# Retention of a hybrid decoder step: own accumulator banks, a third projection bank, and transposes moved into the gate's projection

## The chip, the cores and the metric

One core of a Trainium2 chip. The metric is the device time of one execution in microseconds (us). Engines are called as the profile calls them: PE (matrix products and transposes), PEld (loading of PE's weights), DVE, ACT, POOL, and SP, which issues most DMAs.

## What is computed

One decoder layer on 1,024 prompt tokens and 8 x 4 sample tokens (1,056 token columns in all), float32, width 1,024. The normed input is projected to 6,468 columns; these feed a sparse attention, which picks 256 keys per query by an indexer's scores, and in parallel a retention with 8 heads of 64; both are gated, merged and projected out. The part at stake is retention, per head (lg is the head's log decay, chunks of 128 tokens):

```
scores = einsum('bihd,bjhd->bhij', q, k) * dmat
out = einsum('bhij,bjhe->bihe', scores, v)
out = out + einsum('bihd,bhde->bihe', q, state) * q_decay
new_state = exp(lg * C) * state + einsum('bjhd,bjhe->bhde', k * k_decay, v)
y_r = group_norm_heads(out) * g_ret * silu(zr)
```

## The kernel before, in words

The projection runs in blocks of 128 columns of w_in. `project` takes a block's weights, split by ACT (L195) and DVE or POOL (L196) into a high and a low part, and makes three chunks of 352 tokens; a chunk is 24 products (8 slices of the width x 3 terms, lines 209 to 211) into one PSUM bank, which a function `use` then empties on ACT or DVE. These chunks take two banks by turns (`pj`), so a chunk can start when the one before the last has been emptied.

`retention` goes through four pairs of heads. For each it projects keys, queries (both rotated), values and the gate z; then the attention queries (`split_rows`: ACT L446 and DVE L447 make a high and a low part of each chunk, and after the third chunk ACT L451 copies its last 32 columns to `qs`), then two blocks of merging gates (`gates`, ACT L643). PE has its instructions interleaved by a scheduler that works on the program's order, on data and on `issue_after`, which forbids an instruction to be placed ahead of another.

Inside `pair`: values and keys are turned to tokens (`to_tokens`: 9 transposes each into `pt`, emptied by ACT, L524 and L527). `kd` and `vtok` give the states (L545), a scan on DVE (`S`, L547), two copies on ACT into `SD` (L549). Query-key products go into `pl` (L556), and DVE multiplies them with the decay (`tmp`, L561, 1,024 columns). SD times queries (L568) and values times `tmp` (L571) add up in `po`, which ACT copies (L577), PE turns (L581), ACT copies (L582). The sample tokens do the same in small (L594 to L605, `ss` on DVE, L596). Group norm follows: mean on DVE (L614), a subtraction on POOL (L617), squares on ACT (L619), the rest on DVE and POOL, and three more blocks of transposes (L633).

`pl` is two tiles of two banks each, `pt` two banks, `pj` two: all eight of PSUM.

While PE goes through gates and retention, DVE and ACT search for the 256th largest score (`pick_all`): 31 rounds, one per bit of the threshold. In a round DVE counts five score tiles (L795), ACT counts two by signs (L802: 1,024 columns of 128 rows, then `scs`, the sample's 1,056), DVE makes the bit (L809, L811), the threshold (L871) and the next candidate (`cand`, L873), on which the next counts wait. Their work is in the same two queues as retention's.

```
def count_signs(thr):
    for j, (sc, bi, n, W) in enumerate(AB):
        ...
        nc.scalar.activation(junk[:n, :W], sc, AF.Sign, bias=thr[:n, NV + j:NV + j + 1], scale=-1.0,
```

Of the kernel before, what the change touches and what calls it, by code (L numbers as in the profile page):

```python
# [8 lines left out]
F32 = mybir.dt.float32  # L9
# [108 lines left out]
def _hybrid_step(ctx, tc, A, outs, dbg):  # L118
# [292 lines left out]
    def project(f0, use, chunks=chunks):  # L411

        if not split:
            prefetch()
        g0, w = split.pop(0)
        assert g0 == f0
        prefetch()
        for c, sl in enumerate(chunks):
            p = pj()[:, :sl.stop - sl.start]
            for k in range(KT):  # L420
                terms(p, w, k, sl)
            use(c, p)

    back = []

# [14 lines left out]
    def split_rows(pool, f0, p, dst, new, x=None):  # L440

        hl = [pool.tile([128, TT], F32R, name="raw", bufs=2) for _ in "hl"]

        def use(c, y):
            sl = slice(c * CH, c * CH + CH)
            nc.scalar.copy(hl[0][:, sl], y)  # L446
            nc.vector.tensor_sub(hl[1][:, sl], y, f32(hl[0][:, sl]))  # L447
            if x is not None:
                nc.scalar.copy(x[:, sl], y)
            if c == 2:  # L450
                nc.scalar.copy(new[:, p], y[:, CH - NS:])  # L451
        project(f0, use)
# [7 lines left out]
    def retention(gp):  # L460
        with ExitStack() as s3:
            rp = s3.enter_context(tc.tile_pool(name="rp", bufs=1, reuse_waits="tile"))
            RC = rp.tile([128, R_ALL], F32, name="rc")
            nc.sync.dma_start(RC, A["rcs"])
            O = rp.tile([128, 9, 2, 64], F32, name="O")
            nc.gpsimd.memset(O[:, 8], 0.0)
            SD = rp.tile([128, 8, 128], F32, name="SD")
            nc.gpsimd.memset(SD, 0.0)
            for p in range(4):
                pair(rp, RC, O, SD, p)  # L470
                split_rows(gp, O_QA + 128 * p, p, QD, qs)
                gates(gp, (4 + 2 * p, 5 + 2 * p))

    def big(rp, name):
# [1 line left out]

    def to_tokens(src, use):

        for g in range(3):
# [7 lines left out]
    def pair(rp, RC, O, SD, p):  # L487
# [64 lines left out]

        sT = []
        for g in (0, 1):
            px = pl()
            together([lambda c=c, i=i: nc.tensor.matmul(px[:, 512 * i + 128 * c:512 * i + 128 * c + 128],  # L556
                                                        kT[head[i], 512 * g + 128 * c:512 * g + 128 * c + 128],
                                                        qT[head[i], 512 * g + 128 * c:512 * g + 128 * c + 128], start=True, stop=True)
                      for c in range(4) for i in (0, 1)])
            t = flat(big(rp, "tmp"))[:, :1024].rearrange("p (i c x) -> p i c x", i=2, c=4)  # L560
            nc.vector.tensor_tensor(t, px.rearrange("p (i c x) -> p i c x", i=2, c=4),  # L561
                                    DM[:, M_D:M_D + 256].rearrange("p (i x) -> p i x", i=2).unsqueeze(2).to_broadcast([128, 2, 4, 128]),
                                    op=OP.mult)
            sT.append(t)


        po = pl()
        together([lambda c=c: nc.tensor.matmul(po[:, 128 * c:128 * c + 128], SD[:, c - 1], qT[:, 128 * c:128 * c + 128],  # L568
                                               start=(c % 4 == 3), stop=False) for c in range(7, 0, -1)])
        for g in (0, 1):  # L570
            together([lambda c=c, i=i: nc.tensor.matmul(po[head[i], 128 * c:128 * c + 128], vtok[:, c, head[i]], sT[g][:, i, c % 4],  # L571
                                                        start=False, stop=(c % 4 == 3))
                      for c in range(4 * g, 4 * g + 4) for i in (0, 1)])
        oT = flat(big(rp, "tmp"))[:, :1024]
        for g in (0, 1):
            half = slice(512 * g, 512 * g + 512)
            nc.scalar.copy(oT[:, half], po[:, half])  # L577
            x = pt()
            for j in range(4):
                c0 = 512 * g + 128 * j  # L580
# [11 lines left out]
        px = pl()  # L592
        for i in (0, 1):
            nc.tensor.matmul(px[:NS, 512 * i:512 * i + 32], kT[head[i], T:], qT[head[i], T:], start=True, stop=True)  # L594
        ss = rp.tile([NS, 64], F32, name="ss")
        nc.vector.tensor_tensor(ss.rearrange("p (i t) -> p i t", i=2), px[:NS].rearrange("p (i t) -> p i t", i=2)[:, :, :32],  # L596
                                DM[:NS, M_S:M_S + 64].rearrange("p (i t) -> p i t", i=2), op=OP.mult)
        pi = pl()
        together([lambda b=b, i=i: nc.tensor.matmul(pi[:NS, 512 * i:512 * i + 64], qm[head[i], b], ST0[head[i], b], start=(b == 0), stop=False)
                  for b in range(NB) for i in (0, 1)])  # L600
        for i in (0, 1):
            nc.tensor.matmul(pi[:NS, 512 * i:512 * i + 64], ss[:, 32 * i:32 * i + 32], vtok[:NS, 8, head[i]], start=False, stop=True)
        nc.scalar.copy(O[:NS, 8], pi[:NS].rearrange("p (h e) -> p h e", h=2)[:, :, :64])
# [45 lines left out]
    with ExitStack() as s1:  # L649
# [412 lines left out]
        past_scores(G)  # L1062
    for p in range(4):
        x = tl.tile([128, TT], F32, name="kx", bufs=1)
        split_rows(tl, O_KA + 128 * p, p, KD, ks, x)
# [323 lines left out]
```

## Time and profile before

| | us |
|---|---|
| median of 3 runs | 1141.44 (1141.26 to 1142.6) |
| the profiled execution | 1139.63 |
| its span, first to last instruction | 1137.8 |
| PE busy | 1089.7 (96%) |
| DVE busy | 679.5 (60%) |
| ACT busy | 471.1 (41%) |
| POOL busy | 226.2 (20%) |

Read it so: the four pairs of retention lie between about 165 and 555 us of the span; the head before them loads inputs and makes the scores, the attention follows. A busy share is a mean over these stages. PE's time counts a product until its modelled end, so two products that overlap in the pipe are not counted twice. A wait is the idle time ahead of an instruction, with the instruction that ended it.

### The profile page before, as it was taken

Reading aid. Unit: us, or ns where it says so; the run is one execution under the profiler, and the core shown is the slowest. Engines: PE = TensorE matmul, PEld = TensorE weight load, DVE = VectorE, ACT = ScalarE, POOL = GpSimd, SP = SyncE. Lnnn points to the kernel's source line nnn. Section 1 sums busy time; section 2 is a strip of 40 time slices with the busy share of each in tenths; the row PEclk is TensorE's granted clock in tenths of the full one; section 3 lists DMA queues with packets and bytes.
Section 4 is the critical chain, followed back from the end, with each engine's and each line's share of the span. In section 5 each row is a group of like instructions: output and inputs, shape, how many; then the busy total and the mean of one; then the engine's idle time right before and its main releaser. Section 6 shows DMA issues by size and latency. Waiting matters only on the chain.

```text
span 1137.8 us, 20198 instructions
## 1 busy us (share of the span) xinstructions
PE 1089.7 (96%) x7978; PEld 986.6 (87%) x7978; DVE 679.5 (60%) x1637; ACT 471.1 (41%) x910; POOL 226.2 (20%) x194
## 2 busy tenths in 40 slices
PE   6989999999989999999999999999989999999997
PEld 5779788899879999999989999777989888898886
DVE  6775369999999865943223122101357767588645
ACT  6574355654565332232233322211336666443111
POOL 0012015023310311012332212143013333100000
PEclk9999999999999999999999999999999999999999
DMA  9933334135233524422876676596899741483321
GB/s 311 229 89 94 101 113 133 41 108 153 80 91 108 151 77 131 130 61 78 275 253 211 218 222 175 187 312 225 278 267 256 197 111 31 156 269 118 116 93 56
DMA packets 157237, 179.32 MB, mean 158 GB/s; under 512 B 18821, under 2 KB 129101, under 8 KB 156054
## 3 DMA queue, kind: packets, MB, share of 16 engines
q1 hardware_dynamic: 147208, 142.31, 42.4%
q0 software_dynamic: 9856, 35.66, 9.7%
q8 instruction: 63, 1.03, 0.4%
q14 instruction: 32, 0.26, 0.1%
q10 hardware_dynamic: 78, 0.06, 0.0%
HBM read 137.23 MB, written 36.98 MB: 153 GB/s over the span
## 4 chain that ended last, share of the span: by engine, by line
PE 74%; DVE 12%; DMA 5%; ACT 4%; issue 3%; SPq 1%; DVEq 0%; ACTq 0%
PE pj L209 13%; PE pj L211 13%; PE pj L210 13%; DVE eq L795 4%; PE po L1173 3%; PE pj L1327 3%; PE pj L1326 3%; PE pj L1325 3%; PE str L1014 2%; PE tr L1156 2%; PE pj L949 2%; PE pj L950 2%; PE pj L951 2%; ACT ra L802 2%; PE sx L1042 1%
## 5 line engine op out<-in xcount | busy, mean ns | idle before, releaser
L209 PE MATMUL pj<-hh,wh 128*128 128x352 f32 (+1 forms) x1168 | 384.5, 329 | 10.8 <-ACT qs L451 4.4
L211 PE MATMUL pj<-hh,wl 128*128 128x352 f32 (+1 forms) x1168 | 378.8, 324 | 0.0
L210 PE MATMUL pj<-hl,wh 128*128 128x352 f32 (+1 forms) x1168 | 378.2, 324 | 0.0
L209 PEld LDWEIGHTS pj<-hh,wh 128*128 128x128 f32 x1168 | 220.1, 188 | 20.7 <-issue 8.1
L211 PEld LDWEIGHTS pj<-hh,wl 128*128 128x128 f32 x1168 | 219.9, 188 | 4.8 <-issue 4.1
L210 PEld LDWEIGHTS pj<-hl,wh 128*128 128x128 f32 x1168 | 220.8, 189 | 2.9 <-issue 2.5
L795 DVE TENSOR_SCALAR_CACHE_REDUCE eq<-sc,cand 128x896 bf16<-128x896 f32 (+4 forms) x155 | 135.6, 875 | 2.4
L195 ACT CAST wh<-ws 128x1024 fp32r<-128x1024 f32 (+1 forms) x65 | 61.1, 941 | 115.6 <-PE pj L210 67.7
L196 DVE TENSOR_TENSOR wl<-ws,wh 128x1024 fp32r<-128x1024 f32 (+1 forms) x48 | 51.8, 1082 | 59.3 <-ACT wh L195 59.2
L196 POOL TENSOR_TENSOR wl<-ws,wh 128x1024 fp32r<-128x1024 f32 x17 | 41.4, 2437 | 166.9 <-ACT wh L195 166.7
L1143 POOL TENSOR_SCALAR lg<-lg,st 128x1024 f32<-128x1024 f32 (+7 forms) x64 | 48.2, 759 | 121.6 <-DVE st L1142 73.2
L802 ACT ACTIVATE ra<-sc,cand 128x1024 bf16<-128x1024 f32 x31 | 35.7, 1151 | 59.7 <-DVE cand L873 58.7
L1141 ACT ACTIVATE lg<-lg,st 128x1024 f32<-128x1024 f32 (+7 forms) x64 | 49.5, 775 | 24.7 <-DVE st L1140 22.5
L1016 DVE COPY kt<-str 128x512 f32<-128x512 f32 x32 | 22.1, 690 | 61.2 <-PE str L1014 57.6
L643 ACT ACTIVATE raw<-pj 128x352 f32<-128x352 f32 x48 | 22.2, 462 | 77.7 <-PE pj L211 74.5
L1325 PE MATMUL pj<-woh,MH 128*128 128x512 f32 (+1 forms) x136 | 51.3, 377 | 0.0
L1326 PE MATMUL pj<-wol,MH 128*128 128x512 f32 (+1 forms) x136 | 51.2, 377 | 0.0
L1327 PE MATMUL pj<-woh,ML 128*128 128x512 f32 (+1 forms) x136 | 51.2, 377 | 0.0
L984 POOL DMA_INDIRECT kv<-in_cache_k,idx x32 | 31.0, 968 | 98.5 <-PE str L1014 79.8
L984 POOL DMA_INDIRECT kv<-in_cache_v,idx x32 | 31.1, 972 | 74.5 <-PE sx L1042 45.4
L1156 PE MATMUL tr<-C,lg 128*128 128x128 f32 x288 | 44.5, 276 | 1.2 <-DVE pT L1158 0.3
L1156 PEld LDWEIGHTS tr<-C,lg 128*128 128x128 f32 x288 | 33.7, 140 | 9.5 <-issue 2.4
(352 smaller groups left out, 1956.3 us busy)
## 6 DMA issues: line engine op xcount, KB each, us to landing
ws<-in_w_in SPq DMA_DIRECT2D x51, 512.0 KB
TG<-raw SPq DMA_DIRECT2D x16, 528.0 KB
rot<-in_rot SPq DMA_DIRECT2D x8, 1056.0 KB
x<-in_w_ada SPq DMA_DIRECT2D x16, 512.0 KB
u<-TG SPq DMA_DIRECT2D x8, 528.0 KB
t<-TG SPq DMA_DIRECT2D x8, 528.0 KB
x<-in_x_prompt SPq DMA_DIRECT2D x8, 512.0 KB
out<-tk SPq DMA_DIRECT2D x16, 256.0 KB
```

Source lines behind the costliest of these rows:

```text
L195: nc.scalar.copy(wh[:, :, :n], ws[:, :, :n])
L196: (nc.vector if k == 4 or len(order) % 3 else nc.gpsimd).tensor_sub(wl[:, :, :n], ws[:, :, :n], f32(wh[:, :, :n]))
L209: nc.tensor.matmul(p, wh[:, k], HH[k][:, sl], start=(k == 0), stop=False)
L210: nc.tensor.matmul(p, wh[:, k], HL[k][:, sl], start=False, stop=False)
L211: nc.tensor.matmul(p, wl[:, k], HH[k][:, sl], start=False, stop=(k == KT - 1))
L795: nc.vector.tensor_scalar(junk[:n, :W], sc, thr[:n, j:j + 1], 0.0, op0=op, op1=OP.add, accum_out=cnt[:n, j:j + 1])
L802: nc.scalar.activation(junk[:n, :W], sc, AF.Sign, bias=thr[:n, NV + j:NV + j + 1], scale=-1.0, accum_out=cnt[:n, NV + j:NV + j + 1])
L984: nc.gpsimd.indirect_dma_start(out=t.rearrange("p s c -> p (s c)"), out_offset=None, in_=cache.rearrange("g (r s) h d -> (g r) (s h d)", s ...
L1156: nc.tensor.transpose(x[:, 128 * (j - j0):128 * (j - j0) + 128], lg[:, j % 2, 128 * (j // 2):128 * (j // 2) + 128], ident)
L1325: nc.tensor.matmul(x, MH[:, k, tk], wh[:, k], start=(k == 0), stop=False)
L1326: nc.tensor.matmul(x, MH[:, k, tk], wl[:, k], start=False, stop=False)
L1327: nc.tensor.matmul(x, ML[:, k, tk], wh[:, k], start=False, stop=(k == KT - 1))
```

## The change

Before retention the pool with `pl` and `pt` is closed and one with two `pt`, three single accumulator banks `pb` and one bank `pj3` is opened. `two()` gives two of the `pb`. Every third chunk of a projection takes `pj3`. A double-width tile becomes two single ones, so that its reader on DVE or ACT becomes two instructions. Transposes of values and keys, a group of up to four at a time, stand behind the chunks of z's projection: both large groups of the values behind the first chunk, their small one and the first of the keys behind the second, the rest behind the third. The first chunk of the attention queries' projection now stands ahead of SD's products. Lines of the new file carry other numbers: L451 is L469, L446 L464, L549 L578, L547 L576, L561 L591, L596 L630, L568 L601, L577 L610, L619 L653, L643 L677, L802 L836, L811 L845, L809 L843, L871 L905, L873 L907, L795 L829, L196 L205, L195 L204, L538 L562, L527 L552.

```
+    third, turns = [None], [0]
     def pj():
+        turns[0] += 1
+        if third[0] and turns[0] % 3 == 0:
+            return third[0].tile([128, 512], F32, name="pj3", bufs=1)
         return psj.tile([128, 512], F32, name="pj", bufs=2)
+    def two():
+        return [ps.tile([128, 512], F32, name="pb", bufs=3) for _ in (0, 1)]
...
+    def project_parts(f0, use, chunks=chunks):
...
+            end = last_on(mybir.EngineType.PE)
             use(c, p)
+            yield end
...
             for p in range(4):
-                pair(rp, RC, O, SD, p)
-                split_rows(gp, O_QA + 128 * p, p, QD, qs)
+                rows = split_rows(gp, O_QA + 128 * p, p, QD, qs)
+                pair(rp, RC, O, SD, p, rows)
+                for _ in rows:
+                    pass
...
-        to_tokens(raw(O_VR + 128 * p, "tmp"), use_v)
-        to_tokens(kT, use_k)
+        vT = raw(O_VR + 128 * p, "tmp")
...
-        project(O_ZR + 128 * p, use_z)
+        blocks = [x for a in (turned(vT, use_v), turned(kT, use_k)) for x in (a, a, a)]
+        for c, end in enumerate(project_parts(O_ZR + 128 * p, use_z)):
+            with tc.issue_after(end):
+                for x in blocks[2 * c:2 * c + 2]:
+                    next(x)
...
-            px = pl()
+            px = two()
...
-            nc.vector.tensor_tensor(t, px.rearrange("p (i c x) -> p i c x", i=2, c=4),
...
+            for i in (0, 1):
+                nc.vector.tensor_tensor(t[:, i], px[i].rearrange("p (c x) -> p c x", c=4),
+                                        DM[:, M_D + 128 * i:M_D + 128 * i + 128].unsqueeze(1).to_broadcast([128, 4, 128]), op=OP.mult)
...
-        po = pl()
...
+        end = next(rows)
+
+        po = two()
+        by_bank = lambda c: slice(128 * (c % 4), 128 * (c % 4) + 128)
+        with tc.issue_after(end):
+            together([lambda c=c: nc.tensor.matmul(po[c // 4][:, by_bank(c)], SD[:, c - 1], qT[:, 128 * c:128 * c + 128],
+                                                   start=(c % 4 == 3), stop=False) for c in range(7, 0, -1)])
...
+            nc.scalar.copy(oT[:, half], po[g])
...
+        px = two()
...
+        for i in (0, 1):
+            nc.vector.tensor_tensor(ss[:, 32 * i:32 * i + 32], px[i][:NS, :32], DM[:NS, M_S + 32 * i:M_S + 32 * i + 32], op=OP.mult)
+        pi = two()
...
+        for i in (0, 1):
+            nc.scalar.copy(O[:NS, 8, i], pi[i][:NS, :64])
...
         gates(gp, range(4))
+        ps1.close()
+        ps1 = ExitStack()
+        ps = third[0] = ps1.enter_context(tc.tile_pool(name="psr", bufs=1, reuse_waits="tile", space=PSUM))
         retention(gp)
         drain()
...
+    third[0] = None
     ps1.close()
```

ACT's queue behind pair 1, in round 25 of the search, before (`raw` is the attention queries' high part, then the gates' rows; `sc` and `scs` are the two sign passes):

```order
L195 CAST wh<-ws 128x1024
L446 CAST raw<-pj 128x352
L802 ACTIVATE ra,cnt<-sc_787,cand 128x1024
L451 COPY qs<-pj 128x32
L619 ACTIVATE tmp<-O 128x1152
L802 ACTIVATE ra,cnt<-scs,cand 32x1056
L643 ACTIVATE raw<-pj 128x352 x2
```

and the same place in the change (`pj_3118` is the third bank):

```order
L204 CAST wh<-ws 128x1024
L464 CAST raw<-pj_3118 128x352
L836 ACTIVATE ra,cnt<-sc_787,cand 128x1024
L836 ACTIVATE ra,cnt<-scs,cand 32x1056
L653 ACTIVATE tmp<-O 128x1152
L469 COPY qs<-pj_3118 128x32
L677 ACTIVATE raw<-pj 128x352 x2
```

The copy to `qs`, which frees the bank, moved behind the second sign pass and the squares of the same round.

DVE's queue at pair 1's state scan, before, from the third gate chunk on:

```order
L538 SCALAR_TENSOR_TENSOR zsT<-zt,zsT 128x352
L561 TENSOR_TENSOR tmp<-pl,dm 128x1024
L871 TENSOR_TENSOR base<-base,inc 128x7
L547 SCALAR_TENSOR_TENSOR S<-dm,pt 128x512
L873 TENSOR_SCALAR cand<-base 128x7
L795 TENSOR_SCALAR eq,cnt<-sc_786,cand 128x896
L561 TENSOR_TENSOR tmp<-pl,dm 128x1024
```

and in the change:

```order
L562 SCALAR_TENSOR_TENSOR zsT<-zt,zsT 128x352
L591 TENSOR_TENSOR tmp<-pb,dm 128x512 x2
L905 TENSOR_TENSOR base<-base,inc 128x7
L591 TENSOR_TENSOR tmp<-pb,dm 128x512
L907 TENSOR_SCALAR cand<-base 128x7
L829 TENSOR_SCALAR eq,cnt<-sc_786,cand 128x896
L576 SCALAR_TENSOR_TENSOR S<-dm,pt 128x512
L845 TENSOR_SCALAR inc<-cnt 128x1
L829 TENSOR_SCALAR eq,cnt<-sc_785,cand 128x768
L591 TENSOR_TENSOR tmp<-pb,dm 128x512
```

The scan moved behind three half products, the new candidate and one count; the last half product follows behind the next count.

ACT's queue at the copies of that scan into `SD`, before:

```order
L527 COPY kd<-pt 32x128
L549 COPY SD<-S 64x8x64 x2
L802 ACTIVATE ra,cnt<-sc_787,cand 128x1024
L802 ACTIVATE ra,cnt<-scs,cand 32x1056
L446 CAST raw<-pj 128x352
```

and in the change:

```order
L552 COPY kd<-pt 32x128
L836 ACTIVATE ra,cnt<-sc_787,cand 128x1024
L836 ACTIVATE ra,cnt<-scs,cand 32x1056
L578 COPY SD<-S 64x8x64 x2
L464 CAST raw<-pj 128x352
```

The two copies moved behind both sign passes of the round.

## Rows read from the trace of the kernel before

**Rows 1.** The page, part 1: busy time, share of the span, instructions.
```profile
PE 1089.7 (96%) x7978; PEld 986.6 (87%) x7978; DVE 679.5 (60%) x1637; ACT 471.1 (41%) x910; POOL 226.2 (20%) x194
```

**Rows 2.** Waits of PE, 148 to 560 us: line waited for, total, times, longest.
```profile
PE pj L209 <- ACT qs L451: 4.4, 2, 2.2
PE pt L484 <- ACT tmp L499: 3.1, 2, 2.1
PE pj L209 <- DVE raw L447: 1.7, 1, 1.7
PE pl L568 <- ACT SD L549: 1.5, 2, 1.0
PE pj L209 <- ACT zsT L537: 1.4, 1, 1.4
PE pj L209 <- ACT qrT L499: 1.2, 1, 1.2
```

**Rows 3.** Timeline of PE: start us, length us, instruction, [idle before, releaser].
```profile
151.88 0.32 PE L209 MATMUL pj<-hh,wh 128*128 128x352 f32 x1
...
163.33 0.32 PE L209 MATMUL pj<-hh,wh 128*128 128x352 f32 x1
...
339.29 0.43 PE L209 MATMUL pj<-hh,wh 128*128 128x352 f32 x1 [2.21 <-ACT qs L451]
...
414.18 1.72 PE L568 MATMUL pl<-qrT,SD 128*128 128x128 f32 x14
```

**Rows 4.** Busy time by stretch: us, engine busy (instructions), PE clock, DMA share, GB/s.
```profile
180.00:260.00 80.00, 74.86 (x560) 70.68 (x559) 77.33 (x196) 45.63 (x82) 19.15 (x10) 1.00 0.32 93
...
285.00:350.00 65.00, 58.05 (x443) 53.89 (x443) 62.73 (x155) 37.04 (x68) 14.39 (x8) 0.97 0.27 83
```
The engines stand in the order PE, PEld, DVE, ACT, POOL.

**Rows 5.** The same view for the stretch of the lower clock.
```profile
296.60:300.00 3.40, 3.40 (x14) 3.28 (x13) 3.11 (x10) 1.47 (x4) 0.00 (x0) 0.51 0.21 46
```

**Rows 6.** Timeline of ACT, in round 25 and at pair 2's state copies.
```profile
337.93 1.15 ACT L802 ACTIVATE ra<-sc,cand 128x1024 bf16<-128x1024 f32 x1 [5.34 <-DVE cand L873]
...
339.08 0.16 ACT L451 COPY qs<-pj 128x32 f32<-128x32 f32 x1
339.14 1.17 ACT L619 ACTIVATE tmp<-O 128x1152 f32<-128x1152 f32 x1
340.21 1.16 ACT L802 ACTIVATE ra<-scs,cand 32x1056 bf16<-32x1056 f32 x1
...
411.14 2.40 ACT L549 COPY SD<-S 64x512 f32<-64x512 f32 x2 [1.15 <-DVE S L547]
```

**Rows 7.** Timeline of DVE: instructions that the sum prices, rounds 22 to 26, pair 2.
```profile
314.93 1.22 DVE L561 TENSOR_TENSOR tmp<-pl,dm 128x1024 f32<-128x1024 f32 x1
...
322.23 0.21 DVE L596 TENSOR_TENSOR ss<-pl,dm 32x64 f32<-32x64 f32 x1
...
326.72 1.15 DVE L795 TENSOR_SCALAR_CACHE_REDUCE eq<-sc,cand 128x896 bf16<-128x896 f32 x1
...
329.77 0.74 DVE L608 SCALAR_TENSOR_TENSOR st<-st,rc,pt 128x512 f32<-128x512 f32 x1
...
335.33 2.30 DVE L871 TENSOR_TENSOR base<-base,inc 128x7 int32<-128x7 int32 x1
...
344.19 0.17 DVE L871 TENSOR_TENSOR base<-base,inc 128x7 int32<-128x7 int32 x1
...
408.56 0.50 DVE L538 SCALAR_TENSOR_TENSOR zsT<-zt,zsT 128x352 f32<-128x352 f32 x1
```

**Rows 8.** Waits of DVE, 150 to 395 us: total, times, longest.
```profile
DVE inc L811 <- ACT ra L802: 5.2, 18, 1.5
DVE qrT L513 <- DMA tmp<-qrT: 1.7, 1, 1.7
DVE tmp L636 <- PE pt L633: 0.7, 1, 0.7
```

**Rows 9.** Timeline of POOL in the same stretch.
```profile
335.23 2.38 POOL L196 TENSOR_TENSOR wl<-ws,wh 128x1024 fp32r<-128x1024 f32 x1
```

More of the change, by code (lines that the diff above doesn't have):

```diff
@@ L409, in prefetch, with last_on @@
                 split.append((f0, wsplit(wp, wload(wp, w_in, f0, 128), 128)))
-    def project(f0, use, chunks=chunks):
+    def last_on(engine):
+        return next(i for i in reversed(nc.cur_bb.bb.instructions) if i.engine == engine)
+    def project_parts(f0, use, chunks=chunks):
         if not split:
@@ L421, in project @@
                 terms(p, w, k, sl)
+            end = last_on(mybir.EngineType.PE)
             use(c, p)
+            yield end
+    def project(f0, use, chunks=chunks):
+        for _ in project_parts(f0, use, chunks):
+            pass
     back = []
@@ L451, in use @@
                 nc.scalar.copy(new[:, p], y[:, CH - NS:])
-        project(f0, use)
+        yield from project_parts(f0, use)
         for d, t in zip(dst, hl):
@@ L469, in retention @@
             for p in range(4):
-                pair(rp, RC, O, SD, p)
-                split_rows(gp, O_QA + 128 * p, p, QD, qs)
+                rows = split_rows(gp, O_QA + 128 * p, p, QD, qs)
+                pair(rp, RC, O, SD, p, rows)
+                for _ in rows:
+                    pass
                 gates(gp, (4 + 2 * p, 5 + 2 * p))
@@ L477, in to_tokens, with turned @@
     def to_tokens(src, use):
+        for _ in turned(src, use):
+            pass
+    def turned(src, use):
         for g in range(3):
@@ L485, in to_tokens, with pair @@
             use(4 * g, m, 128 if g < 2 else NS, p)
-    def pair(rp, RC, O, SD, p):
+            yield
+    def pair(rp, RC, O, SD, p, rows):
         flat = lambda t: t.rearrange("p t c -> p (t c)")[:, :TT]
@@ L560, in pair @@
             t = flat(big(rp, "tmp"))[:, :1024].rearrange("p (i c x) -> p i c x", i=2, c=4)
-            nc.vector.tensor_tensor(t, px.rearrange("p (i c x) -> p i c x", i=2, c=4),
-                                    DM[:, M_D:M_D + 256].rearrange("p (i x) -> p i x", i=2).unsqueeze(2).to_broadcast([128, 2, 4, 128]),
-                                    op=OP.mult)
+            for i in (0, 1):
+                nc.vector.tensor_tensor(t[:, i], px[i].rearrange("p (c x) -> p c x", c=4),
+                                        DM[:, M_D + 128 * i:M_D + 128 * i + 128].unsqueeze(1).to_broadcast([128, 4, 128]), op=OP.mult)
             sT.append(t)
-        po = pl()
-        together([lambda c=c: nc.tensor.matmul(po[:, 128 * c:128 * c + 128], SD[:, c - 1], qT[:, 128 * c:128 * c + 128],
-                                               start=(c % 4 == 3), stop=False) for c in range(7, 0, -1)])
+        end = next(rows)
[4 more added lines that the diff above has]
+                                                   start=(c % 4 == 3), stop=False) for c in range(7, 0, -1)])
         for g in (0, 1):
-            together([lambda c=c, i=i: nc.tensor.matmul(po[head[i], 128 * c:128 * c + 128], vtok[:, c, head[i]], sT[g][:, i, c % 4],
+            together([lambda c=c, i=i: nc.tensor.matmul(po[g][head[i], by_bank(c)], vtok[:, c, head[i]], sT[g][:, i, c % 4],
                                                         start=False, stop=(c % 4 == 3))
@@ L576, in pair @@
             half = slice(512 * g, 512 * g + 512)
-            nc.scalar.copy(oT[:, half], po[:, half])
+            nc.scalar.copy(oT[:, half], po[g])
             x = pt()
@@ L591, in pair @@
                                     RC[:NS, R_MB:R_MB + 8].unsqueeze(2).to_broadcast([NS, NB, 64]), op=OP.mult)
-        px = pl()
+        px = two()
         for i in (0, 1):
-            nc.tensor.matmul(px[:NS, 512 * i:512 * i + 32], kT[head[i], T:], qT[head[i], T:], start=True, stop=True)
+            nc.tensor.matmul(px[i][:NS, :32], kT[head[i], T:], qT[head[i], T:], start=True, stop=True)
         ss = rp.tile([NS, 64], F32, name="ss")
[L596 to L599, printed above, removed]
+        for i in (0, 1):
+            nc.vector.tensor_tensor(ss[:, 32 * i:32 * i + 32], px[i][:NS, :32], DM[:NS, M_S + 32 * i:M_S + 32 * i + 32], op=OP.mult)
+        pi = two()
+        together([lambda b=b, i=i: nc.tensor.matmul(pi[i][:NS, :64], qm[head[i], b], ST0[head[i], b], start=(b == 0), stop=False)
                   for b in range(NB) for i in (0, 1)])
         for i in (0, 1):
-            nc.tensor.matmul(pi[:NS, 512 * i:512 * i + 64], ss[:, 32 * i:32 * i + 32], vtok[:NS, 8, head[i]], start=False, stop=True)
-        nc.scalar.copy(O[:NS, 8], pi[:NS].rearrange("p (h e) -> p h e", h=2)[:, :, :64])
+            nc.tensor.matmul(pi[i][:NS, :64], ss[:, 32 * i:32 * i + 32], vtok[:NS, 8, head[i]], start=False, stop=True)
+        for i in (0, 1):
+            nc.scalar.copy(O[:NS, 8, i], pi[i][:NS, :64])
         pn = pt()
@@ L1064, in _hybrid_step @@
         x = tl.tile([128, TT], F32, name="kx", bufs=1)
-        split_rows(tl, O_KA + 128 * p, p, KD, ks, x)
+        for _ in split_rows(tl, O_KA + 128 * p, p, KD, ks, x):
+            pass
         token_rows(tl, x, p, k_out, ks_out, None)
```

2 lines of the change are left out of this document (1 added, 1 removed).

## The prediction

> **What bounds the kernel now.** I read the page first, then the stretches, then PE's waits, then the instructions on either side of the last of them. PE is busy 96% of the span [rows 1], so time is won only where PE stands still or is behind. Between 148 and 560 us, which holds the four pairs of retention, PE waits 13.3 us in all (4.4 + 3.1 + 1.7 + 1.5 + 1.4 + 1.2), and every releaser is ACT or DVE, no DMA [rows 2]. All of it lies before 339.3 us, the last wait being the 2.21 us that end at 339.29 [rows 3]; pairs 2 and 3 run without one. Why there: in 180:260 DVE is busy 77.33 of 80 us and in 285:350 62.73 of 65 [rows 4], because the search for the 256th score (31 rounds, on DVE and ACT) fills both engines. PE's waits in pairs 0 and 1 are waits for ACT and DVE to come round to retention's small instructions between two pieces of search.
>
> A second loss lies in the same place: from 296.6 to 300.0 us the granted clock is 0.51 [rows 5], the lower of its two levels, right behind a wait of PE. A product of the projection takes 0.159 us at the upper level (72 of them from 151.88 to 163.33 us) [rows 3].
>
> **The change, part by part.** The pool is reopened with two transpose banks, three accumulators and one bank more for projections. The order of the instructions shows that every third chunk, and only that, uses the new bank.
>
> *The third bank.* PE's wait for a bank is now a wait for the chunk three before, not two: 24 products more, 24 x 0.159 = 3.8 us of slack. Four of the six waits are of this kind: 4.4 (L451), 1.7 (L447), 1.4 (L537) and 1.2 (qrT), 8.7 us [rows 2]. Taken alone they would go, none being over 2.2 us long.
>
> *What is late next.* The order answers it: the search's rounds are unchanged, and almost every instruction of retention on ACT and DVE stands in the same round as before, so it comes when the search lets it. The last wait decides, because PE runs free behind it. Before, PE stood at the second chunk of a gate until ACT's L451 copied the last columns of the queries' third chunk, in round 25. In the change the second chunk finds a bank free and PE goes on to the third, where it waits for the same copy (L469). That is worth 24 products, **+3.82 us**. But L469 now stands behind the second sign pass and the squares: 340.21 - 339.14 = 1.07 us for the squares and 1.16 for the pass [rows 6], **-2.23 us**. And DVE comes to round 25 later, by what the edits add ahead of it. Eight products of 512 columns stand for four of 1,024 at 1.22 us: a half costs at least 0.61 us, half a whole, and at most the 0.74 of L608, which reads 512 columns from PSUM [rows 7]; I take 0.66, nearer to the same instruction, so 8 x 0.66 - 4 x 1.22 = 0.40 (0 to 1.04). Four small products stand for two of 0.21 us [rows 7], at most 0.21 each: +0.4. Together **-0.8 us** (0.1 to 1.5).
>
> PE must be there by then, and is. Its previous wait would be for the second small product (L630), in round 24 behind the 896-column count that ended at 327.87 us [rows 7]: with 0.8 us more, 328.7, then some 1.5 us of small products and 61 products x 0.159 = 9.7, so 339.9 us. The copy comes at 339.24 + 2.23 + 0.8 = 342.3 us. PE then stands where it stood at 339.29 + 3.82 = 343.1 us. **Sum: 3.82 - 2.23 - 0.8 = 0.8 us gained.**
>
> *Transposes moved.* PE does the same 18 a pair. Those of the values now all follow the gate projection's first chunk and wait for the third values chunk, copied by ACT (the 3.1 us wait [rows 2]) in the same round; before, five of the nine stood ahead of those 24 products. So here PE arrives earlier by five transposes and waits longer: nothing gained, nothing lost, since both end with that copy.
>
> *Accumulators.* Only three banks take the place of two double ones. The last four of 16 key-query products of a pair wait for DVE's first half product; in pairs 0 and 1 that is one more wait for the search, and PE waits at L469 afterwards anyway, so it shortens that wait and costs nothing of its own. SD's two copies on ACT follow both sign passes in place of one, 1.16 us later [rows 6], covered by the projection chunk that now stands ahead of their reader. If that cover is short by a microsecond, PE's later wait at L469 is shorter by as much.
>
> *The rest.* One ACT copy more a pair and the halved instructions in pairs 2 and 3 lie under PE, which has no wait there [rows 2]. On SP, state loads and query stores change places in two pairs and a weight load overtakes three mask copies; nothing of pairs 0 and 1 waits for a DMA [rows 2]. POOL's order is unchanged.
>
> The profiled execution took 1139.63 us (1137.8 and 1.83 around it); the sum gives 1138.8. The median of the runs stands 1.81 us above it, so the forecast is 1141.44 - 0.8 = **1140.6 us**. A change under 0.2%, 2.3 us, is about what a measurement of this kernel cannot tell from none.
>
> **The rivals.**
>
> *Faster: the waits really go.* If ACT and DVE serve PE in time, PE keeps the 8.7 us, and the lower clock of [rows 5] may not come. The Trainium skill (Perfetto Trace Analysis, Optimizing Tensor Performance) advises that independent groups of products rotate through different PSUM banks, so that emptying one overlaps the next; by that rule the waits go and this case follows. Row and rule differ in whose turn it is: here the emptying engine is full. Even so the gain ends at pair 2. There the state copies started at 411.14 us, 2.40 us long, and their reader on PE at 414.18 [rows 3, 6]. In the change one product of the gate (0.50) and three halves (2.0) more stand ahead of the scan, plus the 0.8: 414.4. DVE's own waits would shrink: 1.7 for qrT, 0.7 for PE, the longest 1.5 of those for ACT [rows 8], 3.9 in all: copies at 410.5, reader at 412.9, 1.3 us sooner, and with 20 more products done ahead of it (36 between the gate's last chunk and this reader, before 16), 3.2 us. Gain 4.5 us, **1136.9 us**; with none of the 1.5, 3.0. For it: slack of 3.8 us against waits of 2.2. Against: L469 and the state copies moved back in ACT's order.
>
> *Slower: the search itself slips.* DVE's small search instructions stop when POOL works: L871 took 2.30 us from 335.33 against 0.17 at 344.19, while POOL's L196 ran from 335.23 to 337.61 [rows 7, 9]. The Trainium skill (SBUF — State Buffer, Who interferes with whom) says the two engines share a port pair that one holds for a whole instruction; the row agrees. Moving retention's instructions against the rounds moves these meetings; one more ahead of round 25 costs 2.13 us. It also lengthens PE's wait, and PE's lower clock followed a wait of 2.1 us at 296.6: 3.4 us at half speed lose 1.7. From a slip of 0.8 us the change is slower; with both, 0.8 - 2.13 - 1.7 = -3.0 us, **1144.4 us**. For it: PE's waits become fewer and longer, 2.4 us at L469. Against: POOL's order and the rounds are as before.
>
> *It does not decouple at all* is the forecast itself.
>
> **How the numbers follow.** Forecast 0.50; it holds from 1139.1 to 1142.5 us, by the bounds of the halves and a microsecond of round timing. Faster 0.27, since slack is real; slower 0.23, since one meeting suffices. Faster by over 0.2% is the first rival, 0.27; within it the forecast, 0.50; slower 0.23. The range reaches past both rivals' times by their bounds, 1135.8 to 1144.8 us.
>
> **What would show it.** After: PE's wait for qs in pair 1 is still there, one chunk later, at some 342 us; waits for zsT, raw and qrT are gone; waits for tmp, SD and the small products are longer; PE's waits in 180:345 sum to 12 us or more. Wrong if that sum falls under 8 us, if PE waits in pair 2, or if DVE reaches round 25 over 2 us later than 337.7 us.

## The result, and the profile after

| | kernel before | changed kernel |
|---|---|---|
| median of 6 runs each | 1141.35 us | 1135.57 us (1133.65 to 1137.38) |
| ratio, 95% interval | | 0.9949 (0.9934 to 0.9965) |
| span of the profiled execution | 1137.8 us | 1133.9 us |

The change is faster by 5.8 us (4.0 to 7.5 by the interval). The forecast said 1140.6 us and a range from 1135.8; the time of the faster rival was 1136.9 us. In later sessions the kernel before had medians between 1137.1 and 1139.3 us, so all kernels below are compared by their ratio to the runs of before on the same chip. One execution, of the kernel with two more counts, took 1530.84 us at a mean granted clock of 0.655 and is in none of the ratios.

The page after, part 1, answers to [rows 1]: PE is again the engine that is never free, and a little busier.

```profile
PE 1094.3 (97%) x7977; PEld 991.6 (87%) x7978; DVE 680.4 (60%) x1649; ACT 471.3 (42%) x914; POOL 227.9 (20%) x194
```

PE's waits between 148 and 560 us, the view of [rows 2]:

```profile
PE pt L508 <- ACT tmp L524: 4.6, 3, 1.9
PE pt L508 <- ACT vtok L549: 1.0, 1, 1.0
PE pt L639 <- ACT O L615: 0.3, 1, 0.3
```

All four waits for a projection's bank (qs, raw, zsT, qrT: 8.7 us) and both for SD are gone; 5.9 us are left of 13.3, nearly all of them for the transposes that the change moved. I had expected 12 us or more, with the wait for qs still there at 342 us; a sum under 8 us was the prediction's own sign of being wrong. The stretch of the lower clock is longer than the one of [rows 5] (columns of [rows 4]); of its 6.8 us PE stands still for 0.8:

```profile
293.40:300.20 6.80, 6.02 (x22) 6.02 (x23) 6.48 (x19) 4.38 (x10) 0.00 (x0) 0.50 0.29 80
```

Where the wait for qs was expected, ACT's timeline shows the copy (now L469) done at 337.1 us, in the order that I had read (behind the sign passes L836 and the squares L653), but 5.2 us sooner than the 342.3 that I had worked out:

```profile
333.45 1.15 ACT L836 ACTIVATE ra<-sc,cand 128x1024 bf16<-128x1024 f32 x1 [1.51 <-DVE cand L907]
...
334.73 1.18 ACT L836 ACTIVATE ra<-scs,cand 32x1056 bf16<-32x1056 f32 x1
...
335.90 1.15 ACT L653 ACTIVATE tmp<-O 128x1152 f32<-128x1152 f32 x1
336.96 0.16 ACT L469 COPY qs<-pj 128x32 f32<-128x32 f32 x1
```

PE came to the chunk that needs this bank at some 338.1 us (61 products behind the small ones, which it left at 328.33) and did not wait. So DVE, which releases that ACT pass with `cand`, was early. Its timeline around the end of round 24 answers to [rows 7]:

```profile
331.17 0.17 DVE L905 TENSOR_TENSOR base<-base,inc 128x7 int32<-128x7 int32 x1
331.37 1.98 DVE L907 TENSOR_SCALAR cand<-base 128x7 int32<-128x7 int32 x1
333.39 1.15 DVE L829 TENSOR_SCALAR_CACHE_REDUCE eq<-sc,cand 128x896 bf16<-128x896 f32 x1
```

and POOL's, to [rows 9]:

```profile
331.21 2.12 POOL L651 TENSOR_TENSOR O<-O,mu 128x1152 f32<-128x1152 f32 x1 [25.41 <-DVE inc L843]
333.29 2.41 POOL L205 TENSOR_TENSOR wl<-ws,wh 128x1024 fp32r<-128x1024 f32 x1
```

One of DVE's three small instructions is held, by POOL's first; POOL's second finds DVE in a count of 896 columns, which takes its usual 1.15 us. Before, two were held in this round: L871 by the weight split [rows 7, 9], and ahead of it L809 by the pass over O:

```profile
333.56 1.74 DVE L809 TENSOR_SCALAR inc<-cnt 128x5 int32<-128x5 f32 x1
```
```profile
333.14 2.12 POOL L617 TENSOR_TENSOR O<-O,mu 128x1152 f32<-128x1152 f32 x1 [28.73 <-DVE mu L615]
```

I add up such holds between 157 and 385 us: for each DVE instruction what it takes over the short length of its own form, where that is over 0.2 us. Each of them lies beside an instruction of POOL. They make **28.6 us before and 23.9 us after**; the last round begins (`cand` of round 30) at 376.87 us before and 372.22 after. The difference of 4.7 us is the same. The groups of the three small instructions (31 rounds) show most of it; before:

```profile
L809 DVE TENSOR_SCALAR inc<-cnt 128x5 int32<-128x5 f32 x31 | 18.8, 606 | 0.9
L871 DVE TENSOR_TENSOR base<-base,inc 128x7 int32<-128x7 int32 x31 | 14.3, 463 | 0.8
...
L873 DVE TENSOR_SCALAR cand<-base 128x7 int32<-128x7 int32 x30 | 7.2, 240 | 0.8
```

and after (40.3 us there, 35.7 here):

```profile
L843 DVE TENSOR_SCALAR inc<-cnt 128x5 int32<-128x5 f32 x31 | 12.6, 406 | 0.8
L905 DVE TENSOR_TENSOR base<-base,inc 128x7 int32<-128x7 int32 x31 | 12.2, 393 | 0.8
L907 DVE TENSOR_SCALAR cand<-base 128x7 int32<-128x7 int32 x30 | 10.9, 362 | 0.8
```

### The profile page after: what moved, and what is told of

Read it like the earlier page. It is cut to its first block, busy times and chain, and to the rows that moved or that the text cites. A ratio compares the mean times of both kernels' runs of the same rounds, so it can differ in the third digit from the quotient of the medians.

```text
span 1133.9 us, 20210 instructions
## 1 busy us (share of the span) xinstructions
PE 1094.3 (97%) x7977; PEld 991.6 (87%) x7978; DVE 680.4 (60%) x1649; ACT 471.3 (42%) x914; POOL 227.9 (20%) x194
## 5 line engine op out<-in xcount | busy, mean ns | idle before, releaser
L829 DVE TENSOR_SCALAR_CACHE_REDUCE eq<-sc,cand 128x896 bf16<-128x896 f32 (+4 forms) x155 | 135.8, 876 | 2.4
L204 ACT CAST wh<-ws 128x1024 fp32r<-128x1024 f32 (+1 forms) x65 | 61.0, 940 | 119.9 <-PE pj L219 62.5
L205 DVE TENSOR_TENSOR wl<-ws,wh 128x1024 fp32r<-128x1024 f32 (+1 forms) x48 | 51.8, 1082 | 70.0 <-ACT wh L204 69.9
L205 POOL TENSOR_TENSOR wl<-ws,wh 128x1024 fp32r<-128x1024 f32 x17 | 40.9, 2403 | 157.0 <-ACT wh L204 156.3
L836 ACT ACTIVATE ra<-sc,cand 128x1024 bf16<-128x1024 f32 x31 | 35.7, 1151 | 66.6 <-DVE cand L907 65.5
L677 ACT ACTIVATE raw<-pj 128x352 f32<-128x352 f32 x48 | 22.2, 462 | 73.0 <-PE pj L220 65.2
```

The costliest lines, as they stand in the source:

```text
L204: nc.scalar.copy(wh[:, :, :n], ws[:, :, :n])
L205: (nc.vector if k == 4 or len(order) % 3 else nc.gpsimd).tensor_sub(wl[:, :, :n], ws[:, :, :n], f32(wh[:, :, :n]))
L829: nc.vector.tensor_scalar(junk[:n, :W], sc, thr[:n, j:j + 1], 0.0, op0=op, op1=OP.add, accum_out=cnt[:n, j:j + 1])
```

## The experiments

Four theories. **A**: the third bank's slack takes the waits. **B**: the search is ready sooner because it meets POOL's long instructions less. **C**: the moved transposes, or the early chunk, earn it for PE by themselves. **D**, formed after the first runs: the bank earns its gain in pairs 0 and 1, and pair 2 decides whether it is kept. All kernels in one table; PE's waits are those between 148 and 560 us, and the last column is when DVE wrote the `cand` that ends round 24.

| kernel | ratio to before (95%) | PE waits, us | holds on DVE, us | round 24 ends |
|---|---|---|---|---|
| before | 1 | 13.3 | 28.6 | 337.8 |
| the change | 0.9949 (0.9934 to 0.9965) | 5.9 | 23.9 | 333.4 |
| change, two banks | 1.0016 (1.0005 to 1.0027) | 10.9 | 26.6 | 336.3 |
| banks only | 1.0003 (0.9990 to 1.0016) | 8.0 | 28.7 | 338.5 |
| change, transposes back | 1.0014 (0.9995 to 1.0032) | 8.1 | 28.6 | 338.1 |
| change, chunk back | 0.9953 (0.9941 to 0.9966) | 6.0 | 23.9 | 333.3 |
| change, pieces | 0.9956 (0.9939 to 0.9973) | 7.5 | 18.0 | 328.4 |
| transposes back, pieces | 0.9905 (0.9887 to 0.9924) | 1.6 | 14.3 | 326.2 |
| before, pieces | 0.9897 (0.9881 to 0.9913) | 9.2 | 19.8 | 328.2 |
| change, heads in turn | 0.9985 (0.9973 to 0.9997) | 10.0 | 29.5 | 336.0 |
| before, late end | 1.0067 (1.0048 to 1.0087) | 18.3 | 26.0 | 339.0 |
| change, late end | 1.0048 (1.0031 to 1.0066) | 12.6 | 22.9 | 333.1 |
| transposes back, late end | 1.0034 (1.0022 to 1.0047) | 12.2 | 30.9 | 339.8 |
| transposes back, pieces, late end | 0.9940 (0.9919 to 0.9961) | 5.7 | 14.4 | 326.5 |
| before, one round | 0.9828 (0.9815 to 0.9840) | 0.2 | | |
| change, one round | 0.9866 (0.9851 to 0.9880) | 0 | | |
| change, one more count | 1.0051 (1.0037 to 1.0065) | 14.4 | 30.6 | 338.0 |
| before, one more count | 1.0011 (0.9998 to 1.0023) | 13.2 | 30.2 | 340.0 |
| change, two more counts | 1.0037 (1.0023 to 1.0051) | | | |
| transposes back, pieces, heads in turn | **0.9858 (0.9842 to 0.9874)** | 3.2 | 17.6 | 326.8 |

(Of the kernel with two more counts no profile is read.)

### Parts of the change taken back

*Two banks:*
```diff
-        ps = third[0] = ps1.enter_context(tc.tile_pool(name="psr", ...
+        ps = ps1.enter_context(tc.tile_pool(name="psr", ...
```


> The changed kernel without the third projection bank: three accumulator banks, moved transposes and the early chunk stay. Theory A (the bank: PE's slack of 24 products takes the waits away): the gain of 5.8 us goes, 1139 to 1142 us, and the waits of projections for raw, zsT, qrT or qs are back with at least 4 us in sum. Theory B (meetings: the search on DVE runs into POOL's long instructions less often, and is ready sooner): near the changed kernel, 1135 to 1138 us, if the end of round 24 stays near 333.4 us; whatever the banks, the time follows that instant. Theory C (the moved transposes and the early chunk): 1135 to 1137 us.

*Transposes back* (and *banks only*, which has both this edit and the next):
```diff
-        vT = raw(O_VR + 128 * p, "tmp")
+        to_tokens(raw(O_VR + 128 * p, "tmp"), use_v)
+        to_tokens(kT, use_k)
...
-        blocks = [x for a in (turned(vT, use_v), turned(kT, use_k)) for x in (a, a, a)]
-        for c, end in enumerate(project_parts(O_ZR + 128 * p, use_z)):
...
+        project(O_ZR + 128 * p, use_z)
```


> The kernel before with the new banks alone (three accumulators, the third bank for projections); transposes and the queries' first chunk stand where they stood. Theory A: all of the gain, 1135 to 1137 us, PE's waits between 180 and 345 us at 6 us or less. Theory B: undecided, it follows the end of round 24 on DVE (337.8 us before, 333.4 in the change). Theory C: little gain, 1139 to 1141 us, with the waits for tmp at a projection's end and for SD still there.

> The changed kernel with the transposes of values and keys back ahead of the gate's projection. Theory A: as the change, 1134.5 to 1136.5 us. Theory C: 1137 us or more, the wait for the third chunk of values (tmp) as long as before, 3.1 us. My prediction held that both places end with the same copy: no difference.

*Chunk back:*
```diff
-        end = next(rows)
...
-        with tc.issue_after(end):
-            together([lambda c=c: nc.tensor.matmul(po[c // 4][:, by_bank(c)], SD[:, c - 1], ...
+        together([lambda c=c: nc.tensor.matmul(po[c // 4][:, by_bank(c)], SD[:, c - 1], ...
```


> The changed kernel with the queries' first chunk back behind the products with SD. Theory A: the two waits for SD are back, 0.6 and 1.0 us before, but PE waits elsewhere less: 1135 to 1137 us. Theory C: 1137 us or more.

Without the bank the waits for qs (4.8 us) and zsT are back and the gain is gone, as A says; with the bank and without the moved transposes the gain is gone too, which A does not say. The early chunk is worth nothing either way. So the change gains nothing without the bank, and the bank gains nothing without the moved transposes. PE's waits with the transposes back:

```profile
PE pt L508 <- ACT tmp L524: 4.5, 2, 3.6
PE pb L582 <- DVE tmp L588: 1.4, 1, 1.4
PE pt L508 <- ACT vtok L549: 1.4, 1, 1.4
PE pt L571 <- ACT kd L552: 0.5, 1, 0.5
PE pb L598 <- ACT SD L575: 0.3, 1, 0.3
```

Here, too, no projection waits for a bank. At the end of pair 1 this kernel is ahead by as much as the change, nearly: the 1,345th product of the projections (all are counted from the first) starts at 350.85 us before, 345.76 in the change and 346.71 here. With two banks it starts at 352.44, although that kernel's round 24 ends sooner than this one's (336.3 against 338.1 us): so it is the bank that earns these microseconds. But pair 2 takes it all back: the 1,849th starts at 447.24 us before, 443.02 in the change, and 447.24 here. PE's timeline and clock in pair 2 show how:

```profile
411.60 1.16 PE L582 MATMUL pb<-qrT,krT 64*128 64x128 f32 x8 [1.44 <-DVE tmp L588]
```
```profile
412.70:416.10 3.40, 3.40 (x14) 3.40 (x14) 1.21 (x3) 0.58 (x2) 0.00 (x0) 0.50 0.32 84
```

PE waits 1.44 us for DVE's mask products, and behind that wait the clock is at its lower level for 3.4 us. DVE is late, and its search has more held instructions than in the change: two in round 24 (below), where the change has one, and one each in rounds 29 and 30 (L840 2.32 and L902 2.40 us), where the change has none:

```profile
334.24 0.95 DVE L840 TENSOR_SCALAR inc<-cnt 128x5 int32<-128x5 f32 x1
335.22 2.33 DVE L902 TENSOR_TENSOR base<-base,inc 128x7 int32<-128x7 int32 x1
```

That is theory D, with B as part of what sets DVE's time. It is not all: the holds are 28.6 us here as before, yet the last round begins at 378.97 us, 2.1 us behind the kernel before.

### POOL's long instructions in pieces

```diff
+            for a in range(0, k, 2):
+                nc.gpsimd.tensor_sub(wl[:, a:a + 2, :n], ws[:, a:a + 2, :n], f32(wh[:, a:a + 2, :n]))
```
and so in four pieces the three steps of the rotation (264 columns each, where POOL has it) and the two passes over O.

> The changed kernel with GpSimd's long instructions (weight splits, rotation, the two passes over the output) in four pieces each, the work the same. In the change's trace DVE's small instructions are held for 23.9 us between 157 and 385 us by instructions of 2.1 to 2.5 us. Theory B (meetings): a hold is at most one piece, some 0.7 us; the holds fall to 6 to 12 us, the search's round 30 ends 12 to 18 us before 372.2 us, and PE's waits between 148 and 560 us fall from 5.9 us; 1127 to 1133 us where the change takes 1135.6. Theory A (PE's own slack in banks is all): the holds may fall, the time stays at 1134 to 1137 us.

> The same pieces in the kernel with three banks and the transposes back ahead of the gate's projection (which was no faster than the kernel before, ratio 1.0014, and had 28.6 us of holds). Theory B: its loss against the change was where GpSimd's instructions met the rounds, so with pieces the loss goes: within 0.15% of the pieces in the changed kernel. Theory C (the place of the transposes counts by itself, for PE): it stays 0.4 to 0.7% slower than the pieces in the changed kernel.

> The same pieces in the kernel before. Theory B: the search is some 15 us shorter, but with two banks PE still waits at the chunk before it is free: faster than the kernel before by 2 to 6 us, and slower than the pieces in the changed kernel by 2 to 5 us (what the third bank is worth by itself). If meetings were all, it would equal the pieces in the changed kernel.

The holds fall by 6 to 14 us in all three, less than I expected, and the search up to the end of round 24 is 2.7 to 9.7 us shorter. The kernel before gains 1.0%, twice what the change brought, without any of its edits; the change itself gains nothing by them (0.9956, where it had 0.9949; its 1132.8 us lies in B's range only because the kernel before took 1137.1 us there). The expectations for the order of the three failed: with pieces the moved transposes are *worse* by 0.5%, where without pieces they were better by 0.65%. So their place has no fixed worth of its own (C falls, with the sign reversed); it shifts retention's and POOL's instructions against the rounds. In the change with pieces PE waits again in pair 2, 2.8 us for DVE, and for the keys' copies 2.6 us, with three stretches of the lower clock (13.6 us in all). PE is 3.2 us ahead of the change at the end of pair 1 (the 1,345th product at 342.58 us), DVE only 2.0 us at its last round (370.22 us): in rounds 25 to 28 DVE stands idle for 4.5 us (0.9 in the change), 2.7 of them for ACT. Why ACT is late there is open. The trace of *before, pieces* is of an execution of 1130.59 us, the slowest of five; their median is 1126.37, so its waits say little of the others.

### The end of the search moved

```diff
+            with tc.issue_after(normed[2].ins):
-            exact(1)
+                exact(1)
...
-            finish(NP - 1)
-
-            with tc.issue_after(normed[2].ins):
+                finish(NP - 1)
```


> The kernel with three banks and the transposes back (ratio 1.0014), and the end of the search (the exact threshold of two blocks and the first of the seven finishes, some 18 us of DVE) behind pair 2's last instruction on DVE, where the other finishes stand. Theory D (the bank earns some 4 us in pairs 0 and 1 with either place of the transposes, and without the moved transposes it is paid back in pair 2, where PE waits 1.4 us for DVE's L588 and runs 3.4 us at the lower clock behind that): the wait of pair 2 goes, ratio 0.995 to 0.997 to the kernel before. Theory C (the transposes themselves earn it): 1.000 to 1.002 as it was.

> The changed kernel with the end of the search behind pair 2. It has no wait of PE in pair 2 to lose: theory D gives the change's own ratio, 0.994 to 0.996, and the same as the kernel with the transposes back and the late end, within 0.15%. Theory C: it stays 0.4 to 0.6% ahead of that one.

> The kernel before with the end of the search behind pair 2. In its trace PE has no wait in pair 2 at all: no gain, ratio 0.999 to 1.001, by theories C and D alike. A gain of over 0.2% would say that the late end is worth something by itself, and that the two runs beside it have to be read against it.

> Three banks, transposes back, GpSimd's instructions in pieces (ratio 0.9905) and the end of the search behind pair 2: its PE waits were 1.6 us in all, 0.4 of them in pair 2. Theory D: 0.4 us less, no more: ratio 0.989 to 0.991, and PE's waits between 148 and 560 us at 1.5 us or less. If the loss in the profile lies elsewhere: a change of over 0.2%.

All four are slower than the same kernels without the edit, against every expectation (with the transposes back by only 0.2%, where the two intervals overlap): DVE's work is then in pair 3, where PE waits 4.6 to 6.5 us at one place (for the mask products in three of them, for the copies into SD in the kernel before). As a test of whole times it failed. Pair 2 by itself agrees with D: with the transposes back its wait is gone, and it takes 97.7 us from the 1,345th product to the 1,849th, where it took 100.5, and the change 97.3.

### Without the search, and with its phase shifted

```diff
-            reached(base, None, -1.0)
+            reached(base, None, 0.0)
...
-            for k in range(30, -1, -1):
+            for k in range(30, 29, -1):
```


> The kernel before with one round of the search in place of 31 (thirty rounds of counting are left out, so the thresholds are not found; all else stays). DVE and ACT are then free in the four pairs. All theories: PE has no or little wait between 160 and 560 us (under 3 us in place of 13.3) and the time falls by 10 to 16 us, to 0.986 to 0.991 of the kernel before.

> The changed kernel with the same single round. If its gain is only that of waits for the search (theories A, B and D), none is left here, and what it adds on PE itself shows: the key-query products of one head behind another, 0.7 us a pair, so 2 to 4 us slower than the kernel before with one round. If the change saves PE time of its own (theory C): faster than that kernel or equal.

These two kernels leave out thirty of the 31 rounds and do not find the threshold. With one round PE has no wait in the four pairs of either kernel (the 0.2 us are behind them), and the change is **slower by 4.5 us** (1123.81 against 1119.26). The kernel before falls by 19.9 us, more than the 10 to 16 expected: by the 2,353rd product it is 18.2 us ahead (524.07 against 542.30 us), where its waits were 13.3 us and its 3.4 us at the lower clock cost some 1.7; the rest is open. The groups of PE between 148 and 545 us show where the change is slower: the key-query products, the sample's small ones, and the turning of the output. Before with one round:

```profile
L556 PE MATMUL pl<-qrT,krT 64*128 64x128 f32 x128 | 10.7, 283 | 0.0
...
L484 PE MATMUL pt<-C,tmp 128*128 128x128 f32 x32 | 4.9, 276 | 0.0
...
L581 PE MATMUL pt<-C,tmp 128*128 128x128 f32 x32 | 4.4, 279 | 0.0
...
L484 PE MATMUL pt<-C,krT 128*128 128x128 f32 x32 | 4.1, 272 | 0.0
...
L594 PE MATMUL pl<-qrT,krT 64*32 64x32 f32 x16 | 1.0, 203 | 0.0
```

the change with one round:

```profile
L585 PE MATMUL pb<-qrT,krT 64*128 64x128 f32 x128 | 12.8, 281 | 0.0
...
L614 PE MATMUL pt<-C,tmp 128*128 128x128 f32 x32 | 5.0, 279 | 0.0
L508 PE MATMUL pt<-C,krT 128*128 128x128 f32 x32 | 4.8, 272 | 0.0
...
L508 PE MATMUL pt<-C,tmp 128*128 128x128 f32 x32 | 4.1, 273 | 0.0
...
L627 PE MATMUL pb<-qrT,krT 64*32 64x32 f32 x16 | 2.0, 203 | 0.0
```

These three groups (L585, L627, L614) make 3.7 us more. The moved transposes make no difference: keys and values together 9.0 us before (L484) and 8.9 here (L508). With the search in place the sign of the change is the other, so the phase of the search was tried by itself:

```diff
+            count(zero, OP.is_ge, [(0, VB[0])])
             for k in range(30, -1, -1):
```


> The changed kernel with one count of 896 columns more on DVE ahead of the rounds (its result is overwritten). It adds 1.15 us of DVE and shifts every round against GpSimd's instructions. If the change's gain stands by itself: 0 to 1.2 us slower than the change, ratio to the kernel before 0.995 to 0.996. If the gain hangs on where the rounds meet GpSimd (theory B): the holds move by over 2 us either way from 23.9, and where they grow PE waits in pair 2 again, ratio 0.998 to 1.002.

> The kernel before with the same count more ahead of the rounds, the control for the change with one more count (1.0051, where the change has 0.9949). If the count is dear by itself, as DVE's work is on the path: the kernel before loses the same, some 1.0 to 1.2%. Theory B: it meets GpSimd in its own way, so it lies anywhere from 0.996 to 1.008, its holds (28.6 us) move by over 1 us, and the difference of the two kernels is another than 0.5%.

> The changed kernel with two counts more. If each count costs by itself: 2.0% over the change, 1.015. Theory B: no such slope; the time follows the holds and the wait of pair 2, 0.995 to 1.010, and may lie below the kernel with one count.

One count of 1.15 us turns a gain of 0.5% into a loss of 0.5%: holds of 30.6 us for 23.9, and PE's waits as before the change, the longest ones for the moved transposes and in pair 2:

```profile
PE pt L508 <- ACT tmp L524: 9.3, 2, 6.2
PE pb L585 <- DVE tmp L591: 3.9, 1, 3.9
PE pb L635 <- DVE ss L630: 0.9, 1, 0.9
PE pb L601 <- ACT SD L578: 0.3, 1, 0.3
```

Behind them the clock is at its lower level in three stretches, 17 us in all, where the change has 6.8. Two counts cost no more than one (1.0037 and 1.0051, the intervals overlap), and the kernel before loses at most 0.2% by the same count (1.0011, an interval that holds 1). It is not the price of DVE's work. The count also let the scheduler turn a few instructions of PE round, so this is a shift of the phase by several small causes, not by 1.15 us alone. With one count in both, the change is the slower one, 1.0051 against 1.0011.

### The heads in turn, and the best version

In the change the second half of the key-query products has four products of each head, two instructions each: it begins with those of one head in the free bank and ends with those of the other, behind DVE. PE's timelines in pair 1 give the price; before, 16 instructions in turn by heads, and after, eight of one head, in the same 1.16 us:

```profile
309.75 1.16 PE L556 MATMUL pl<-qrT,krT 64*128 64x128 f32 x16
```
```profile
311.72 1.16 PE L585 MATMUL pb<-qrT,krT 64*128 64x128 f32 x8
```

The edit makes each product of the second half follow the one before:

```diff
+    def in_turn(products):
+        last = products[0]()
+        for f in products[1:]:
+            with tc.issue_after(last.ins):
+                last = f()
+        return last
...
-            together([lambda c=c, i=i: nc.tensor.matmul(px[i][:, 128 * c: ...
+            (together, in_turn)[g]([lambda c=c, i=i: nc.tensor.matmul(px[i][:, 128 * c: ...
```


> The changed kernel with the second half of the key-query products again in turn by heads. In pair 2 these 32 products took 2.77 us in the change and 2.05 before, since eight at the end are of one head and run one behind the other. If that is the cause: 2.0 to 2.1 us again, 0.7 us a pair, 2.8 us for four pairs where no wait takes it back: 1133 to 1134 us. If the pairs cost the same in turn, or the wait for the bank is longer instead: 1135 to 1137 us.

> The best so far (three banks, transposes back, GpSimd in pieces: ratio 0.9905 and a profile with 1.6 us of PE waits) with the second half of the key-query products in turn by heads. PE is then nearly without waits, so 0.3 to 0.7 us a pair should show: 1 to 3 us less, ratio 0.988 to 0.990. If a wait for the shared bank takes its place in pair 2: 0.990 to 0.994, with a wait for DVE's products of the first half.

In the change itself it lost 0.36%: its holds are 29.5 us, and PE waits 3.1 us in pair 2. On top of banks, transposes back and pieces it is the **best kernel of the study: 0.9858, 1123.12 us where the kernel before took 1139.19**, with no stretch of the lower clock between 148 and 560 us. Its waits there:

```profile
PE pb L615 <- ACT SD L592: 1.6, 2, 1.2
PE pt L520 <- ACT tmp L536: 0.8, 1, 0.8
PE pt L520 <- ACT kd L569: 0.6, 1, 0.6
PE pb L599 <- DVE tmp L605: 0.2, 1, 0.2
```

Against the version without it (0.9905, another session) that is some 5 us, more than the 1 to 3 expected for PE alone. Pair 3, where PE does not wait in any of the four kernels, gives PE's own share: from the 1,849th product to the 2,353rd the edit takes 96.21 us to 95.64 here and 96.02 to 95.34 in the change, 0.6 to 0.7 us a pair and some 2.5 us over four. The rest may be phase; no run here shows it.

## Why the prediction was wrong

**The third bank.** Right in its mechanism: "taken alone they would go", and the four waits of 8.7 us did, with either place of the transposes. The Trainium skill (Perfetto Trace Analysis, Optimizing Tensor Performance) says that independent groups of products should rotate through PSUM banks; by that rule the waits go, and the traces agree (no wait of a projection in either kernel).

**"Transposes moved: nothing gained, nothing lost"** is the step that failed, and with it the last wait of the sum: the copy to qs at 342.3 us and PE there at 339.9. The copy came at 337.1 us, PE at 338.1, and there was no wait. I asked in which round each instruction of ACT and DVE stands, found the rounds the same, and took DVE's times from before with 0.8 us more. With the transposes back that was right: round 24 ends at 338.1 us where I had 338.6. With them moved it ended at 333.4: POOL's pass over O then starts at 331.21 us (333.03 with them back, 333.14 before), and the weight split behind it runs beside a count; against the kernel before, holds fell by 4.7 us, in rounds 6, 16, 20 and 24 above all. The round does not say where in the round POOL is met. Nor is the wait for qs seen in any kernel with the third bank, not even with one more count, where round 24 ends at 338.0 us: there PE had stood 6.2 us for the transposes first.

**Accumulators: "costs nothing of its own".** Wrong: with one round the change costs PE 4.5 us over four pairs. 2.1 of them are the key-query products, whose second half the three banks break by heads, 1.0 the sample's small products, 0.6 the turning of the output, and none the transposes.

**The faster rival** had nearly the right end, in part by luck. It priced pair 2 as the place where the gain stops, put PE's products with SD at 412.9 us, and 4.5 us of gain. The row is at 413.14, before at 414.18 [rows 3]:

```profile
413.14 1.05 PE L601 MATMUL pb<-qrT,SD 128*128 128x128 f32 x8
```

The measured gain is 5.8 us, 3.9 by the two spans. But it took DVE's sooner copies from shorter waits for ACT and PE; the runs show fewer holds. I gave it 0.27 and the forecast 0.50, because L469 stood further back in ACT's order. It did, and did not matter.

**The slower rival** had the right mechanism with the wrong sign for this kernel: meetings with POOL decide, at about the 2.13 us each that it used, but the change had fewer. With one more count it has more, and is slower, 1.0051. The Trainium skill (SBUF — State Buffer, Who interferes with whom) says that only the port pair that DVE shares with GpSimd is locked, for a whole instruction, and exempts the form of tensor_scalar that also writes its accumulator. The rows agree: L907 was held to 1.98 us, L829, which accumulates, took 1.15 beside POOL's split.

**The range** ended at 1135.8 us, 0.2 above the result: it took the faster rival's 1.5 us of shorter ACT waits as the most, and did not let the holds fall, only rise.

So the gain is that of the third bank in pairs 0 and 1, where it brings 3 to 5 us net of PE's own cost (the 1,345th product at 347.95 us with the banks only, 345.76 in the change, 350.85 before), and it is kept only where the search on DVE is done in time for pair 2. The kernels with their parts taken back show this for the phase that the change happens to have; the test of pair 2 by the late end bears it out there, not in the whole time. That the place of the transposes acts by phase, and not by itself, is shown by the pieces, where its sign turns, and by the equal transposes without the search; the change as a whole loses with one more count and without the search.

## What to carry to other kernels

Where two engines share a resource, which round an instruction stands in is not enough: an edit that moves nothing on either can change which of their instructions meet, here by 4.7 us. Before believing a gain of half a per cent beside such a loop, shift its phase once (one more instruction at its start) in both kernels. And cut the long instruction that holds the other engine into pieces first: it brought 1.0% to the kernel before in a dozen lines, and nothing to the change, where the banks brought 0.5% on one phase and nothing on others. The pieces themselves were not tried at a second phase.

## What had not been expected of the hardware

- A small DVE instruction (five to seven columns) that takes 0.17 us alone takes up to 2.4 us beside a POOL instruction of 2.4. In the kernel before, 18 holds made 28.6 us, 16 of them on the search's three small instructions. In four pieces POOL's work takes longer (120.5 us in the best kernel between 148 and 560, 95.9 before), and the holds fall to 14 to 20 us.
- Products of 64 rows in turn by heads run at 16 in 1.16 us, those of one head behind one another at 8. The Trainium skill (TensorE: Matmul & The Clock Gate, Part 3: Packing small matmuls — row/col tiling) says that products in different row groups overlap; the two rows agree.
- The lower level of the clock, for 3.4 or 6.8 us, followed some of PE's waits and not others: it came 1.1 us after a wait of 0.8 us (transposes back, pieces, at 220.0 us), and did not after the 2.17 us that ended at 232.97 in the kernel before. The best kernel has none between 148 and 560 us.
